# The feed-forward's first product on scaled fp16 parts, with weight sums added by transfers

## The chip, the cores and the metric

The kernel runs on one core of one Trainium2 chip. The metric is the device time of one execution in microseconds (us). The engines of the core are PE (TensorE, the matrix engine; its weight loads are listed apart as PEld), DVE (VectorE), ACT (ScalarE), POOL (GpSimd) and SP (SyncE, which here only starts transfers). POOL starts the transfers that cast a type or add to what lies at the destination; these form the software queue. Those started by SP form the hardware queue.

## The reference

Two layers of an encoder over 1024 tokens of width 1024, then a last norm. All inputs and outputs are fp32.

```python
for l in range(DEPTH):                                   # 2
    h = _rmsnorm(x, g_mix[l])
    p = h @ w_in[l]
    ...                                                  # 8 attention heads, and a gated 31-tap filter
    y = concatenate([y_attn, u], axis=-1) @ w_o[l]
    x = x + y
    h2 = _rmsnorm(x, g_ffn[l])
    z = _dwconv(h2 @ w_up[l], w_dw_ffn[l], b_dw_ffn[l])  # 1024 -> 5632, then 3 taps along the tokens
    zg, zv = split(z, 2, axis=-1)
    x = x + (silu(zg) * zv) @ w_down[l]                  # 2816 -> 1024
return _rmsnorm(x, g_final)
```

`h2 @ w_up` is the feed-forward's first product, the one that changes.

## The kernel before, in words

Each layer runs four stages: input projections, attention, output projection (`wo_steps`), and the feed-forward, which has an up part (`up_steps`) and a down part (`down_steps`). A value is carried as a pair of a high part (the value rounded to a shorter type) and a low part (what is left). A product of two pairs is three matmuls: high by high, high by low, low by high. Before, both parts are fp32r, a 32-bit type that PE takes in one pass.

The first product is cut into 22 blocks `f`, each of 128 channels of the gate and 128 of the value. A block's 2 x 2 halves (gate or value; first or second half of the 1024 input columns) meet the 2 x 2 halves of the activations (rows; first or second 512 tokens) in seven products instead of eight, of sums and differences of halves (Strassen's scheme). `ORDER = (1, 5, 6, 3, 7, 2, 4)` is their order within a block. Each of the seven is twelve matmuls of 128x128 weights by 512 columns: four slices of the input, three matmuls each (`product`, L1120). So the stage has 2 layers x 22 x 7 x 12 = 3696 matmuls.

For each product there must be in time:

- the activations' parts (`self.sets[i]`, tiles `b`): made once a layer in `first`, `combine` and `mix`, at the steps of `MIX_AT`; products 1 and 2 use the plain halves, whose low parts POOL subtracts (`pair`, L1499);
- the weights' parts (tiles `w`): halves that are used as they are (1, 2, 4) arrive by a casting transfer (`cast_pair`, L894), which makes the high part; `complete` then makes the low part by ACT (L189) and an adding transfer (L190). For sums of halves (5, 6, 3, 7) the raw weights `wu` are fetched as fp32 by SP (`fetch`), DVE forms the sums in place by four subtractions or additions (`combine`, L1069), and `part` makes the two parts (L1087, L1497, L1499, L190);
- a free bank of PSUM. `evict` takes the results out by ACT copies and DVE additions into `zg` and `zv`.

After its products, a block goes through the 3-tap filter: `filter_start` is one ACT operation over 1024 tokens (L1505), each `filter_tap` one DVE operation of 1023 columns (L1511), two for the gate (tile `o`) and two for the value (tile `v`); then `silu` on ACT and `close`, a DVE multiplication, whose result is stored by SP. Beside the blocks, `sum_load`, `sum_step` and a store prepare eleven pairs of sums of the down-projection's weights (tiles `sd`, four DVE operations each) from block 7 on.

The order is written out by hand. `feed` walks through the steps; step `n` emits the matmuls of one product (or of two output tiles in `wo_steps`, which has 16 steps), and then everything that was `put` at step `n`, in order of rank. Each engine runs its instructions in this order; only the transfers' places on SP's queue follow from when their waits and buffers allow. So an operation that waits holds up all that stands behind it on its engine. The first four blocks (`LEFT`) are interleaved according to `START`, as the parts of the activations for products 5, 3, 6, 7 and 4 are made only then. From block 4 on (step 44 on) each block takes seven steps.

In `value_squares` and `value_scale` attention finds a power of two as scale for its values: a matmul with ones (tile `vf0p`, L870) sums squares over partitions, and three small DVE operations work on the exponent bits.

Of the kernel before, what the change touches and what calls it, by code (L numbers as in the profile page):

```python
# [71 lines left out]
P_SCALE = 32768.0  # L72
TURNED_BY_DMA = ()
# [17 lines left out]
START += [(i, f + g) for i, g in ((5, 0), (3, 0), (6, 0), (5, 2), (7, 0), (3, 2), (4, 0), (6, 2), (7, 2)) for f in (0, 1)]  # L91
START += [(1, LEFT), (4, 2), (4, 3)]
MIX_AT = (18, 20, 20, 21, 24, 25, 28, 29, 30, 31)
# [3 lines left out]
TAIL_STEPS = 6  # L97
ENDS = (slice(512, 768), slice(768, T))
LEAD_HEADS = 3
FIRST_AT = (0,0,1,1,2,2,3,3)  # L100
EVICT = {(5, 2): 30, (5, 3): 31, (6, 2): 38.295, (6, 3): 39.295, (7, 2): 40.295, (7, 3): 41.295, (5, 0): 24, (5, 1): 25, (1, 2): 35, (1, 3): 36, (2, 2): 36, (2, 3): 37}
# [24 lines left out]
class Encoder:  # L126
# [257 lines left out]
    def run(self):  # L384
# [4 lines left out]
        self.ones = self.cp.tile([128, 128], F32, name="ones")  # L389
        nc.vector.memset(self.ones, 1.0)  # L390
        self.ones_r = self.cp.tile([128, 128], F32R, name="ones_r")
# [9 lines left out]
    def first_sections(self, l, supply):  # L401
# [58 lines left out]
        nc.vector.tensor_copy(out=self.ones_r, in_=self.ones)  # L460
# [87 lines left out]
    def project(self, l, carry):  # L548
# [261 lines left out]
        for i in range(2):  # L810
            held = lambda: launch(query_rope(0), len(seq) - 6)
            add(f"u{i}", "u2", ranked("u2", i, QL, f"u{i}", cqs), lambda i=i: query_rope(1) if i else iter(()), held if i else norm)
        scales = {1: lambda: st.update(squares=self.value_squares(l, w["v"])),
                  2: lambda: st.update(scale=self.value_scale(l, st.pop("squares")))}
# [43 lines left out]
    def value_squares(self, l, w):  # L858
        f = self.cp.tile([128, 8], F32, name=f"vf{l}", tag="vf", bufs=1)
        for k in range(2):  # L860
            t = self.blk(f"vsq{l}_{k}")[:, 0:512]
            self.nc.scalar.activation(out=t, in_=w[0][:, k * 512:(k + 1) * 512].bitcast(F32), func=AF.Square,
                                      scale=self.par[l][:, P_GKV + k:P_GKV + k + 1], accum_out=f[:, k:k + 1])
        return f

    def value_scale(self, l, f):
        nc = self.nc
        ps = self.bank(f"vf{l}p", (128, 1))
        for k in range(2):
            nc.tensor.matmul(ps, self.ones, f[:, k:k + 1], start=k == 0, stop=k == 1)  # L870
        h, s, r = (f[:, i:i + 1] for i in (2, 3, 4))
        nc.vector.tensor_scalar(out=h.bitcast(I32), in0=ps.bitcast(I32), scalar1=24, scalar2=None, op0=ALU.logical_shift_right)
        nc.vector.tensor_scalar(out=s.bitcast(I32), in0=h.bitcast(I32), scalar1=-8388608.0, scalar2=200 * 8388608.0, op0=ALU.mult, op1=ALU.add)
        nc.vector.tensor_scalar(out=r.bitcast(I32), in0=h.bitcast(I32), scalar1=8388608.0, scalar2=39 * 8388608.0, op0=ALU.mult, op1=ALU.add)
        return s, r
# [42 lines left out]
    def load_y(self, l, x, c, k):  # L918
        t = self.blk(f"y{l}_{c}{k}")
        for e in range(2):  # L920
            m = k + 4 * e
            x[m, c] = t[:, HALVES[e]]
            self.nc.sync.dma_start(out=x[m, c], in_=self.xd[l][m][:, HALVES[c]])
# [9 lines left out]
    def wo_steps(self, l, conv, ys, w, casts, x, steps, put):  # L933
        nc, a, par = self.nc, self.a, self.par[l]
        left, right = HALVES
        casts, ps, acc, sq, rf, us = {(1, m): e for m, e in casts.items()}, {}, {}, {}, {}, []
        sets = self.sets = defaultdict(list)

        def load_x():
            for c in range(2):  # L940
                for k in range(4):
                    if (k, c) not in x:
                        self.load_y(l, x, c, k)
# [52 lines left out]
        def norm(c, k):  # L996
            xk = x[k, c]
            nc.vector.scalar_tensor_tensor(out=xk, in0=xk, scalar=par[:, P_GFFN + k:P_GFFN + k + 1], in1=rf[c],
                                           op0=ALU.mult, op1=ALU.mult)

        def first(k):
            norm(0, k)
            i = 1 + k // 4
            sets[i].append(self.pair(x[k, 0], f"b{l}_{i}{k}", "m", True))

        def combine(i, ks, srcs):
            for o, p, q in srcs:
                if q is not None:
                    nc.vector.tensor_tensor(out=o, in0=p, in1=q, op=ALU.subtract)
            pairs = [self.tmp("b", f"b{l}_{i}{k}", F32R, (128, 2, 512)) for k in ks]  # L1010
            for t, src in zip(pairs, srcs):
                nc.scalar.copy(out=t[:, 0], in_=src[0])
            for t, src in zip(pairs, srcs):
                if i in MIX_ADDED:
                    self.complete(None, t[:, 0], t[:, 1], src[0])
                else:
                    nc.vector.tensor_tensor(out=t[:, 1], in0=src[0], in1=t[:, 0].bitcast(F32), op=ALU.subtract)
            sets[i] += pairs
# [23 lines left out]
        for k in range(8):  # L1042
            at = norm_at + FIRST_AT[k]
            put(at, 3, lambda k=k: first(k))
        put(17, 1, lambda: root(1))
        put(18, 0.9, lambda: spread(1))
        b11, b12 = (lambda k, c=c: x[k, c] for c in range(2))
        b21, b22 = (lambda k, c=c: x[k + 4, c] for c in range(2))
        plan = ((5, 0, b11, b12, b11), (3, 4, b22, b22, None), (6, None, b11, b22, b11), (7, None, b12, b22, b12),
                (4, None, b21, b21, b11))  # L1050

        def mix(i, j, o, p, q, ks):
            for k in ks if j is not None else ():
                norm(1, k + j)
            combine(i, ks, [(o(k), p(k), q(k) if q else None) for k in ks])
# [886 lines left out]
```

## Time and profile before

| | us |
|---|---|
| median of 3 runs (2276.03 to 2276.38) | 2276.29 |
| the profiled execution | 2276.63 |
| its span, first to last instruction | 2274.9 |
| up part, first layer (504 to 926) | 422 |
| up part, second layer (1632 to 2052.8) | 420.8 |
| output projection, first layer (406 to 504) | 98 |
| PE busy in the span | 2264.2 |
| DVE busy | 1738.7 |
| ACT busy | 1298.0 |
| POOL busy | 783.0 |

The granted clock of PE was 0.999 over the span. A row of a group of instructions reads: line, engine, operation, tiles written and read (block numbers left out), shapes and type, count, then busy time in us, mean duration in ns, and the idle time of the engine just before them with what ended it. Durations of matmuls overlap, as they are pipelined: the time that one costs is the distance from its start to the next start. DVE's operations overlap a little too.

### The profile page before, as it was taken

How to read it: one execution, taken by the hardware profiler on the slowest of the kernel's cores; microseconds unless marked ns; L12 is line 12 of the kernel's file. 1: busy time of each engine (PE TensorE's matmuls, PEld its weight loads, DVE VectorE, ACT ScalarE, POOL GpSimd, SP SyncE). 2: the span in 40 equal slices, each digit the busy share in tenths (PEclk: the TensorE clock that was granted, in tenths of full speed). 3: DMA queues.
4: the chain of work that ended last, by engine and by line, in shares of the span. 5: the costliest groups of instructions: out<-in, count | busy, mean ns of one | idle time of the engine just before them, and what ended most of it. 6: DMA issues, size and time to landing. Idle time of an engine off the chain costs nothing.

```text
span 2274.9 us, 30440 instructions
## 1 busy us (share of the span) xinstructions
PE 2264.2 (100%) x10690; PEld 1834.8 (81%) x10690; DVE 1738.7 (76%) x2305; ACT 1298.0 (57%) x2058; POOL 783.0 (34%) x812
## 2 busy tenths in 40 slices
PE   9999999999999999999999999999999999999999
PEld 8887777788888888888888877777888888888888
DVE  7989888868877676776559788887697777768765
ACT  5355977646655555544533578784475555555444
POOL 1222797532333333001412237963323333320032
PEclk9999999999999999999999999999999999999999
DMA  6888998856899998935968999867669999989356
GB/s 194 168 180 260 199 207 177 212 151 141 208 281 297 275 297 203 333 106 144 207 139 167 215 255 201 188 150 208 174 132 231 269 300 278 294 208 320 105 121 171
DMA packets 199144, 475.72 MB, mean 209 GB/s; under 512 B 27232, under 2 KB 35280, under 8 KB 198992
## 3 DMA queue, kind: packets, MB, share of 16 engines
q0 software_dynamic: 103136, 222.46, 48.6%
q1 hardware_dynamic: 95568, 250.80, 32.9%
q8 instruction: 84, 1.38, 0.3%
q14 instruction: 68, 0.56, 0.1%
q10 hardware_dynamic: 288, 0.53, 0.1%
HBM read 309.29 MB, written 80.40 MB: 171 GB/s over the span
## 4 chain that ended last, share of the span: by engine, by line
PE 93%; issue 2%; DVE 2%; DMA 1%; ACT 1%; SPq 0%; POOL 0%; DVEq 0%; POOLq 0%; ACTq 0%
PE p L1120 36%; PE pd L1308 18%; PE po L931 7%; PE s L1564 7%; PE t L1604 4%; PE o L1627 4%; PE pq L226 3%; PE pa L226 3%; PE pkv L226 2%; PE pg L226 2%; PE pg L545 2%; PE pa L545 1%; PE pk L226 1%; PE pn L226 1%; PE pkr L759 1%
## 5 line engine op out<-in xcount | busy, mean ns | idle before, releaser
L1120 PE MATMUL p<-b,w 128*128 128x512 f32 x3552 | 807.0, 389 | 0.6 <-DVE zv L1069 0.5
L1120 PEld LDWEIGHTS p<-b,w 128*128 128x128 f32 x3552 | 666.3, 188 | 140.6 <-DVE zv L1069 0.9
L1308 PE MATMUL pd<-ab,wd 128*128 128x512 f32 (+1 forms) x1920 | 422.2, 381 | 0.0
L1308 PEld LDWEIGHTS pd<-ab,wd 128*128 128x128 f32 x1920 | 350.8, 188 | 69.4 <-DVE ab L1499 0.4
L190 POOL DMA_DIRECT2D w<-wu x96 | 84.8, 886 | 360.5 <-ACT w L189 310.0
L1564 PE MATMUL s<-k,q 96*128 96x512 f32 x768 | 207.7, 406 | 0.8 <-ACT p L1574 0.8
L1607 DVE SCALAR_TENSOR_TENSOR pt<-t,pt 128x512 f16<-128x512 f32 x256 | 164.8, 684 | 38.9 <-ACT pt L1606 38.3
L1796 POOL TENSOR_TENSOR late<-gate,par 128x1014 f32<-128x1014 f32 (+12 forms) x79 | 171.6, 2172 | 12.4 <-PE pn L226 12.4
L1606 ACT ACTIVATE pt<-t 128x512 f16<-128x512 f32 x256 | 139.2, 596 | 57.0 <-PE t L1604 56.0
L1511 DVE SCALAR_TENSOR_TENSOR o<-zg,par,o 128x1023 f32<-128x1023 f32 x88 | 112.8, 1283 | 76.5 <-ACT o L1505 75.2
L190 POOL DMA_DIRECT2D w<-in_w_up x116 | 100.5, 867 | 199.2 <-ACT w L189 175.3
L1566 DVE TENSOR_REDUCE mx<-s 128x1 f32<-128x1024 f32 x128 | 155.7, 1217 | 1.3 <-PE s L1564 1.3
L1564 PEld LDWEIGHTS s<-k,q 96*128 96x128 f32 x768 | 135.2, 189 | 23.6 <-ACT p L1574 1.3
L1574 ACT ACTIVATE p<-s,mx 128x1024 f32<-128x1024 f32 x128 | 143.2, 1118 | 4.4 <-DVE mx L1566 4.0
L1779 DVE SCALAR_TENSOR_TENSOR conv<-gate,par,conv 128x1009 f32<-128x1009 f32 (+7 forms) x112 | 142.3, 1274 | 3.7 <-ACT conv L607 1.0
L1604 PEld LDWEIGHTS t<-ident,p 128*128 128x128 f32 x1024 | 119.8, 141 | 25.2 <-DVE yt L1634 0.8
L894 POOL DMA_DIRECT2D wd<-in_w_down x44 | 32.8, 754 | 306.6 <-PE pd L1308 306.4
L1497 ACT CAST ab<-ac 128x512 fp32r<-128x512 f32 x130 | 80.1, 617 | 97.5 <-DVE ac L1243 94.8
L189 ACT ACTIVATE w<-w 128x512 fp32r<-128x512 f32 x212 | 133.5, 630 | 3.0
L1627 PE MATMUL o<-pt,v 128*128 128x512 f16 x512 | 132.8, 381 | 1.2 <-DVE pt L1607 1.1
L1604 PE MATMUL t<-ident,p 128*128 128x128 f32 x1024 | 133.2, 273 | 0.1
L1069 DVE TENSOR_TENSOR zg<-p,zg 128x512 f32<-128x512 f32 x88 | 60.5, 690 | 95.1 <-PE p L1120 88.4
(2117 smaller groups left out, 4083.9 us busy)
## 6 DMA issues: line engine op xcount, KB each, us to landing
w<-in_w_up POOLq DMA_DIRECT2D x232, 256.0 KB, 7.3
wu<-in_w_up SPq DMA_DIRECT2D x88, 512.0 KB, 5.7
w<-wu POOLq DMA_DIRECT2D x96, 256.0 KB, 5.9
sd<-in_w_down SPq DMA_DIRECT2D x44, 512.0 KB, 9.9
ws<-sd SPq DMA_DIRECT2D x44, 512.0 KB, 7.0
wd<-in_w_down POOLq DMA_DIRECT2D x88, 256.0 KB, 5.4
act<-v SPq DMA_DIRECT2D x36, 512.0 KB, 5.8
ac<-act SPq DMA_DIRECT2D x72, 256.0 KB, 6.1
```

Of the source, the lines that this page charges most:

```text
L190: self.nc.gpsimd.dma_start(out=lo, in_=src, accum_op=ALU.add)
L226: nc.tensor.matmul(ps[:, HALVES[c]], w, x[:, HALVES[c]], start=(k == 0 and s == 0), stop=(k == n - 1 and s == 2))
L931: self.nc.tensor.matmul(ps, p[:, sl], q[:, cs], start=(k == 0 and t == 0), stop=(k == 3 and t == 2))
L1120: nc.tensor.matmul(ps, w[p][:, k * 128:(k + 1) * 128], b[:, q], start=(i in (1, 5, 2) and k == 0 and t == 0), stop=(k == 3 and t == 2), sk ...
L1308: nc.tensor.matmul(ps[t, m][:, cs], w[i, j][p][:, m * 128:(m + 1) * 128], b[:, q, cs], start=(i in (1, 5, 2) and j == 0 and s == 0), stop= ...
L1564: nc.tensor.matmul(ps[:, cs], q[i][0:96, qs], k[j][0:96, cs], start=(s == 0), stop=(s == 2))
L1566: nc.vector.tensor_reduce(out=mx, in_=ps, op=ALU.max, axis=AX.X, negate=True)
L1574: nc.scalar.activation(out=p, in_=ps, func=AF.Exp, bias=mx, accum_out=st["sums"][:, qt:qt + 1])
L1604: nc.tensor.transpose(tp[:, i, qi * 128:(qi + 1) * 128], st["p"][2 * qp + qi][:, kt * 128:(kt + 1) * 128], self.ident)
L1607: nc.vector.scalar_tensor_tensor(out=lo, in0=tp, scalar=P_SCALE, in1=hi, op0=ALU.mult, op1=ALU.subtract)
L1627: nc.tensor.matmul(po, v[2 * c + i][:, h // 2, e, :], pt[s][:, 2 * (c % 2) + i, :], start=(c == 0 and i == 0 and s == 0), stop=(c == 3 and ...
L1796: self.nc.gpsimd.tensor_tensor(out=p[:, lo:hi], in0=u[:, lo + s:hi + s], in1=self.tap(l, j, t).broadcast_to([128, hi - lo]), op=ALU.mult)
```

## The change

- The parts of activations and weights for the seven products are fp16 instead of fp32r. The weights are multiplied by a power of two per block before they are split, the activations by one per layer (`gs`, from the norm's gains); the results are multiplied back in `evict` (`back`, and `nback` where the sign is turned).
- The power of two of a block comes from its sum of squares: ACT squares both raw halves with an accumulator (`own_squares`), one fp32 matmul with ones sums over partitions (`own_total`, a matmul of two columns in PE's stream), and five small DVE operations work on the exponent bits (`own_scale`). The first four blocks share one such matmul a layer (`first_total`), within the output projection. Attention's `value_scale` becomes `scales`, with one matmul and more small operations.
- The raw weights of all halves are fetched by SP. Sums of halves are made in place by four adding transfers a block on POOL (`sum5`, `sum6`, `sum3`, `sum7`) instead of DVE operations. High parts are ACT operations with a scale (`upper`), low parts DVE operations with a scale (`lower`); there are no casting transfers and no `complete` in this stage.
- Signs of some sums are turned, so that additions do; `evict` and the down part's `combine` and `evict` follow.
- Activations: tiles of rows `2k` and `2k+1` lie side by side, so that one operation makes parts of two; their low parts are all DVE's.
- `START` is reordered: products 1 and 2 of blocks 0 to 3, then 5, 3, 6, 7 and 4, each of blocks 0 to 3. `MIX_AT` and `EVICT` follow. The filters of blocks 0 to 3 start at the steps of `TAPS_AT`: 36, 39, 42, 46 (gate) and 44, 48, 52, 57 (value). `SUM_AT` sets the down sums' steps after product 1.

The places in the order for block `f` of 4 and above, in steps from its first product: fetch -18, squares -15 and -14, total -13, its scale -12, then high and low parts by `UP`.

```diff
+START += [(i, f) for i in (5, 3, 6, 7, 4) for f in range(LEFT)]
...
+TOTAL_AT = 32
+TAPS_AT = (36, 39, 42, 46), (44, 48, 52, 57)
+UP = {'fetch': -18, 'squares': -15, 'total': -13, 1: (-2, -2), 5: (-10, -9), 6: (-5, -4), 3: (0, 1), 7: (2, 3), 4: (-1, 0)}
+SUM_AT = (0, 1, 2, 6)
...
+        def begin(i, e, src, tag):
+            two = self.tmp(tag, f"b{l}_{i}{e}", F16, (128, 2, 2, 512))
+            src = src.rearrange("p (e c) -> p e c", e=2)
+            nc.scalar.copy(out=two[:, :, 0], in_=src)
+            half[i, e] = two, src
+            sets[i] += [two[:, e] for e in range(2)]
+
+        def end(i, e):
+            two, src = half.pop((i, e))
+            nc.vector.tensor_tensor(out=two[:, :, 1], in0=src, in1=two[:, :, 0], op=ALU.subtract)
...
-        def combine(f, o, p, q, op=ALU.subtract):
-            z = quarters(f)
-            sub(z[o], z[p], z[q], op)
...
+        def block(f, e, h):
+            return a["w_up"][l, f + e * NF][:, HALVES[h]]
+
+        def add_in(dst, src):
+            nc.gpsimd.dma_start(out=dst, in_=src, accum_op=ALU.add)
+
+        def sum5(f):
+            add_in(raw[f][1][:, left], block(f, 1, 1))
...
+        def squares(f, e, out):
+            t = self.blk(f"wsq{l}_{f}{e}", F16)
+            nc.scalar.activation(out=t, in_=raw[f][e], func=AF.Square, accum_out=out)
+
+        def scales(ps, out, w):
+            ps = ps.rearrange("p (f e) -> p f e", e=2)
+            scale, back, nback, v, h = (out[:, i * w:(i + 1) * w] for i in range(5))
+            nc.vector.tensor_reduce(out=v, in_=ps, op=ALU.add, axis=AX.X)
+            self.half_exponent(h, v)
+            self.power(scale, h, -1.0, 204.0)
...
+        def first_total():
+            ps = self.bank(f"wt{l}", (128, 2 * LEFT))
+            tags = self.banks[1][0]
+            tags.insert(0, tags.pop())
+            nc.tensor.matmul(ps, self.ones, st["sums"], start=True, stop=True)
...
+        def own_total(f):
+            st["total", f] = self.pp.tile([128, 2], F32, name=f"wt{l}_{f}", tag=f"d{6 + (f > LEFT and (f + 1) % 2)}", bufs=1)
+            nc.tensor.matmul(st["total", f], self.ones, st["sums", f][:, 6:8], start=True, stop=True)
...
+        def upper(t, src, f):
+            nc.scalar.activation(out=t, in_=src, func=AF.Copy, scale=scale[f])
+
+        def lower(t, src, hi, f):
+            nc.vector.scalar_tensor_tensor(out=t, in0=src, scalar=scale[f], in1=hi, op0=ALU.mult, op1=ALU.subtract)
...
         def evict(i, f):
-            z = st[f]
+            z = zs[f]
+            by = nback[f] if i in (5, 7, 4) else back[f]
+            copy = lambda o, src: nc.scalar.activation(out=o, in_=src, func=AF.Copy, scale=by)
+            plus = lambda o, src: nc.vector.scalar_tensor_tensor(out=o, in0=src, scalar=by, in1=o, op0=ALU.mult, op1=ALU.add)
...
         for f in range(LEFT, NF):
-            n = at[1, f]
+            n = m = at[1, f]
             for e in range(2):
-                put(n - 8, 5, lambda f=f, e=e: fetch(f, 1 - e))
-            put(n - 5, 3, lambda f=f: combine(f, 0, 0, 2))
-            put(n - 4, 3, lambda f=f: combine(f, 2, 2, 3, ALU.add))
...
+                at_step(m + UP["fetch"], 5 + e / 10, fetch, f, e, "b" if e else "wr")
+                at_step(m + UP["squares"] + e, 2, own_squares, f, e)
+            at_step(m + UP["squares"] + 1, 2.1, sum5, f)
+            at_step(max(m + UP["total"], TOTAL_AT), 0.4, own_total, f)
+            at_step(max(m + UP["total"], TOTAL_AT) + 1, 0.5, own_scale, f)
+            for i in (5, 6, 3, 7, 4):
+                hi, lo = (max(m + o, TOTAL_AT + 1) for o in UP[i])
+                at_step(hi, 3.6, part_hi, i, f)
+                at_step(lo, 3.7 if hi == lo else 3.5 if i != 6 else 1, part_lo, i, f)
+                if i in (5, 6):
+                    at_step(lo, 3.75, (sum6, sum3)[i - 5], f)
+            at_step(n + UP[1][0], 1, first_hi, f)
+            at_step(n + UP[1][1], 2, first_lo, f)
+            at_step(n + UP[1][1] + 1, 2, sum7, f)
+            at_step(m + 3, 9, raw.pop, f)
```

299 lines of the change are left out of this document (169 added, 130 removed).

## The prediction, made before the changed kernel was run

> **What bounds the kernel now.** I read the page first (busy shares, slices, the chain that ended last), then the busy time by stretch, then the instructions in order of time. Each engine's row gives busy time, share of the span, and instructions.
>
> ```profile
> PE 2264.2 (100%) x10690; PEld 1834.8 (81%) x10690; DVE 1738.7 (76%) x2305; ACT 1298.0 (57%) x2058; POOL 783.0 (34%) x812
> PE 93%; issue 2%; DVE 2%; DMA 1%; ACT 1%; SPq 0%; POOL 0%; DVEq 0%; POOLq 0%; ACTq 0%
> PE p L1120 36%; PE pd L1308 18%; PE po L931 7%; PE s L1564 7%; PE t L1604 4%; PE o L1627 4%; PE pq L226 3%; PE pa L226 3%; PE pkv L226 2%; PE pg L226 2%; PE pg L545 2%; PE pa L545 1%; PE pk L226 1%; PE pn L226 1%; PE pkr L759 1%
> L1120 PE MATMUL p<-b,w 128*128 128x512 f32 x3552 | 807.0, 389 | 0.6 <-DVE zv L1069 0.5
> L1120 PEld LDWEIGHTS p<-b,w 128*128 128x128 f32 x3552 | 666.3, 188 | 140.6 <-DVE zv L1069 0.9
> 504.00:926.00 422.00, 421.40 (x1862) 348.11 (x1861) 313.84 (x404) 244.08 (x374) 125.38 (x165) 1.00 0.92 245
> 1632.00:2052.80 420.80, 420.80 (x1862) 348.12 (x1862) 314.00 (x404) 244.09 (x374) 123.95 (x165) 1.00 0.92 246
> ```
>
> The stage that changes is the up-projection, L1120. The last two rows are its two passes: length, then busy time of PE, PEld, DVE, ACT and POOL, granted clock, DMA share. PE is busy throughout and stands still 0.6 us before a matmul of L1120 in the whole run. So PE's spacing sets the stage, and whatever else is hidden stays hidden only while its turn comes in time: DVE is at 74% of the pass, DMA at 92%.
>
> **What one matmul costs.** These are instructions in order of time: start, length, engine, line, count.
>
> ```profile
> 298.86 1.02 PE L1627 MATMUL o<-pt,v 128*128 128x512 f16 x4
> 299.72 0.71 PE L1604 MATMUL t<-ident,p 128*128 128x128 f32 x5
> 699.68 4.70 PE L1120 MATMUL p<-b,w 128*128 128x512 f32 x20
> L1627 PEld LDWEIGHTS <-v 128*128 128x128 f16 x512 | 41.7, 98 | 64.3 <-issue 29.2 <-DVE yt L1634 1.0 <-DVE pt L1607 0.6
> ```
> ```profile
> 190.73 0.61 PE L226 MATMUL pn<-cqs_2l,wu10h 128*128 128x512 f32 x2
> 191.18 0.50 PE L870 MATMUL vf0p<-vf,ones 128*128 128x1 f32 x4
> 191.54 0.72 PE L226 MATMUL pn<-cqs_0h,wu10h 128*128 128x512 f32 x2
> 191.92 0.15 DVE L872 TENSOR_SCALAR vf<-vf0p 128x1 int32<-128x1 int32 x1
> 192.10 0.63 PE L226 MATMUL pn<-cqs_0h,wu10l 128*128 128x512 f32 x2
> ```
>
> Twenty matmuls of L1120 take 4.70 us, the last alone 0.389: (4.70-0.389)/19 = 0.2269 us from start to start. Four fp16 matmuls of the same shape start at 298.86 and the next work at 299.72: 0.86/4 = 0.215 us, by the rounding of the starts 0.2125 to 0.2175. I take 0.216. Between 190.73 and 192.10 lie four such fp32r matmuls (0.908) and two fp32 matmuls (four records): 1.37-0.908 = 0.462, so 0.231 us for one fp32 matmul with one or two columns. DVE reads its result 0.24 us after it ended (191.68 to 191.92).
>
> **The change, part by part.**
>
> *Products in fp16.* 2 layers x 22 blocks x 7 products x 12 = 3696 matmuls by 0.2269-0.216 = 0.0109: **-40.3 us**, all on the path. A weight load is 98 ns in fp16 against 188 here; both are shorter than the matmul. Bounds: 0 if long runs stay at 0.227, -53 at 0.2125. I take the fp16 row, being of the same shape.
>
> *Totals for the scales.* 18 blocks a layer each get one fp32 matmul in PE's stream: 36 x 0.231 = **+8.3 us**. Five small DVE operations follow it (0.15 each, row 191.92), 0.75 a block, and two squares on ACT. The first four blocks share one total in the output-projection stage; the next bank there waits for DVE to read it, 0.24+0.15+0.06 = 0.45, with 0.23 for the matmul; the attention's scale takes one matmul instead of two (-0.23). **+0.9** for both layers.
>
> *Weight sums and parts.* Gone: four DVE subtractions a block (L1069 `wu`) and the casting transfers with their corrections; new: four adding transfers a block into the raw weights, ACT makes every high part and DVE every low part. POOL issues four instead of eight. Durations and spacings of DVE:
>
> ```profile
> 701.12 0.69 DVE L1069 TENSOR_TENSOR wu<-wu,wu 128x512 f32<-128x512 f32 x1
> 701.72 1.28 DVE L1511 SCALAR_TENSOR_TENSOR v<-zv,par,v 128x1023 f32<-128x1023 f32 x1
> 702.92 0.69 DVE L1069 TENSOR_TENSOR sd<-sd,sd 128x512 f32<-128x512 f32 x1
> 703.52 0.69 DVE L1069 TENSOR_TENSOR wu<-wu 128x512 f32<-128x512 f32 x1
> L1069 DVE TENSOR_TENSOR v<-v,o 128x1024 f32<-128x1024 f32 x44 | 53.6, 1217 | 0.1
> L998 DVE SCALAR_TENSOR_TENSOR y<-y,par,rf 128x512 f32<-128x512 f32 x16 | 11.3, 745 | 4.0 <-ACT rf L993 4.0
> L1505 ACT ACTIVATE o<-zg,par 128x1024 f32<-128x1024 f32 x44 | 54.2, 1232 | 15.4 <-DVE zg L1069 12.4 <-DMA w<-wu 2.6 <-DMA ws<-sd 0.4
> L1574 ACT ACTIVATE p<-s,mx 128x1024 f32<-128x1024 f32 x128 | 143.2, 1118 | 4.4 <-DVE mx L1566 4.0
> L1574 ACT ACTIVATION_READ_ACCUMULATOR p<-s,mx 128x1 f32 x128 | 26.8, 209 | 0.0
> ```
>
> Successive starts give 0.60 us for 512 columns and 1.20 for a tap; a scaled one (745 long) then 0.66, a product of 1024 columns 1.14. A steady block after: five low parts 3.3, the pair of products 1 and 2 1.2, three evictions 1.98, four taps 4.8, closing 1.14, scale 0.75 = 13.2; with the down-projection's sums (4 x 0.60) 15.6. PE takes 84 x 0.216+0.23 = 18.37 a block (19.06 now). DVE stays under it in sum, but two chains are tight.
>
> (1) Product 7's low part. Its DVE turn, from the end of the total's matmul: 0.24 to the read, 0.75 scale, tap 1.2, sum 0.6, low part of 6 of the next block 0.66, tap 1.2, itself 0.75 = 5.4, gaps 0.1. PE needs it two products of 2.59 later plus two matmuls of 0.216, 5.6. It fits by 0.1 in blocks with sums, by 0.7 in others: at most 0.2 a block, 0 to 4 us over 22 such blocks.
>
> (2) A loop through the raw weights' buffer: product 7's low part frees it, the transfer of three blocks ahead goes in (L), ACT squares it (about 1.25 from start to start, of 1.118 and 0.209), ACT starts the gate's filter of this block behind that (1.23), and DVE has from its first tap to the next low part of 7: four taps 4.8, four low parts 2.64, an eviction 0.66, scale 0.75, three sums 1.8 = 10.65. Together 13.1+L, against 18.37: it waits where L is over 5.2 us (7.0 without sums). L by issue, with the stretch each is from (share of DMA in the rows after):
>
> ```profile
> wu<-in_w_up SPq DMA_DIRECT2D x88, 512.0 KB, 5.7
> w<-wu POOLq DMA_DIRECT2D x96, 256.0 KB, 5.9
> ```
> ```profile
> wu<-in_w_up SPq DMA_DIRECT2D x9, 512.0 KB, 6.3
> q0 software_dynamic: 5671, 10.34, 53.6%
> q1 hardware_dynamic: 4668, 16.98, 49.7%
> ```
> ```profile
> wu<-in_w_up SPq DMA_DIRECT2D x4, 512.0 KB, 5.3
> 650.00:742.00 92.00, 92.00 (x407) 76.17 (x407) 67.12 (x85) 50.74 (x77) 27.75 (x36) 1.00 1.04 298
> 850.00:905.00 55.00, 55.00 (x245) 45.54 (x244) 38.07 (x46) 29.67 (x46) 16.31 (x22) 1.00 0.84 212
> ```
>
> The 6.3 is from 650 to 742, with DMA at 1.04; the 5.3 from 850 to 905, at 0.84. After the change the software queue moves 1 MB a block instead of 2; its five adds and three casts fill 53.6% now, so four adds fill 27% (if a cast costs the same) to 43% (if casts cost nothing); the plain transfers stay near 52% of the shorter block. That makes 0.79 to 0.95, and I take the lower half, 0.84. So I take L = 5.3 as the middle: half of 22 blocks are later, by perhaps 0.5 us (from the 1.0 between the two medians): 11 x 0.5 = **+5.5 us**, chain (1) within it. Ends: 0 (L never above 5.2) and 22 x 1.1 = +24 (L stays 6.3).
>
> The queues: on SP the transfer that waits for its buffer has the loads of the down-projection's sums and the stores of finished blocks behind it; the stores are read only in the next stage. On POOL each add waits for a DVE low part and has the next adds behind it. From the low part to the next high part lie four products (10.4) for the sums of 6 and 3, three (7.8) for 7, against an issue of 0.9 and the 5.9 us of `w<-wu`: spare 3.6 and 1.0, and 7's own low part comes a product later. Nothing, unless an add takes over 8 us.
>
> [...]
>
> *Order, and taps put off.* The first four blocks' filters move behind product start: in steps 47 to 56 (ten products, 25.9 us of PE) DVE has ten taps 12, four closings 4.6, five evictions 3.3, nine widths of low parts 6.0 to 7.0, a scale 0.75: 26.7 to 27.6 by spacings, about 30 by full durations. It falls 1 to 4 us behind, and since low parts of products 6 and 7 queue behind those taps, PE waits for them. I take 3.5 a layer, **+7 us**; ends 0 (slack of the steps before) and 12.
>
> *Activations' parts, evictions with scales, paired loads.* The POOL subtractions go to DVE (the second row: busy times of the first output projection):
>
> ```profile
> L1499 POOL TENSOR_TENSOR b<-y,b 128x512 fp32r<-128x512 f32 x16 | 24.2, 1625 | 28.1 <-ACT b L1497 28.1
> 406.00:504.00 98.00, 97.29 (x452) 78.83 (x451) 67.30 (x104) 46.36 (x74) 38.73 (x42) 1.00 0.67 184
> ```
>
> Two of those become one DVE operation of 1.2 us at the stage's start; PE's spacing there (2.59 a product) leaves DVE about 2 us ahead, so I cost it at nothing; uncovered it would be 4 x 1.2 a layer. The eight early squares on ACT (1.25 each) lie in the output projection, where ACT is busy 46 of 98 us; nothing either, uncovered 1 us.
>
> Sum, against the profiled execution's own 2276.63 (span 2274.9 and 1.7 around it, 0.34 above the median of the runs): -40.3+8.3+0.9+5.5+7 = -18.6, so **2258.0 us**.
>
> **Rivals.**
>
> *No waits.* DVE and transfers always arrive: -40.3+8.3+0.9 = -31.1, so 2245.5. For it: before, PE stands only 0.6 us on L1120 although DMA is full. Against: DVE has less room now.
>
> *The buffer loop decides (slower).* In blocks with sums the period becomes 13.1+L. The gain, 31.1 less 7 = 24, is spent when it exceeds 18.37 by 24/22 = 1.1, at L = 6.4; at L = 7.3 it costs 22 x 2.03 = 45, giving 2245.5+7+45 = 2297. For it: the 6.3 median with sums, DMA full there. Against: a MB less a block.
>
> *The put-off taps cost much more*: one product's time (2.59) lost in each of blocks 4 to 6 beyond my 7, 15.5 in both layers: 2273.5. For it: 30 us of DVE work by durations against 25.9; against: 26.7 by spacings.
>
> *No faster stream* (the change doesn't do what it says). Long fp16 runs keep 0.227: 2276.6+8.3+0.9 = 2285.8, and up to 12.5 of waits, fewer in longer blocks: 2290. Against: only runs of four, but hundreds of them, all near 0.215.
>
> [...]
>
> **How the numbers follow.** My case (5 to 20 us of waits) 0.52; no waits 0.18; taps 0.12; loop 0.12; no faster stream 0.05; the page's 131 ns 0.01. A difference under 0.2% is 4.6 us, about what separates a change from none here. My case and no waits lie below 2271.7, as does a third of the taps' case and the 0.01; the loop's case is slower in most of its range and within the bound in the rest, as is the taps' case. So faster 0.79, same 0.06, slower 0.15. The range leaves out a last tenth on either side: 2243 to 2281.
>
> **What would show it.** L1120's spacing near 0.216 with weight loads near 98 ns. One two-column matmul a block, 0.23 us each. Idle time of PE before the products: some 12 us, released by DVE low parts, in the first 60 us of the stage (7) and in blocks with sums (5.5); DVE waits for the gate's filter start, ACT for `wu` transfers. I am wrong if that idle time exceeds 30 us, if landing in the sum blocks stays over 6 us, or if waits stand in the output projection.

## The result, and the profile after

The changed kernel takes 2266.23 us (median of 5 runs, 2263.01 to 2266.99) against 2276.29 before (5 runs, 2276.03 to 2276.78). The ratio is 0.9953, with a 95% interval of 0.9938 to 0.9967: 10 us faster, where 18 were forecast. The profiled execution took 2264.85.

First the page of the changed kernel: busy times of the engines, the chain that ended last, and the groups that answer to those of before.

```profile
span 2263.0 us, 30127 instructions
PE 2233.7 (99%) x10762; PEld 1511.4 (67%) x10762; DVE 1809.0 (80%) x2484; ACT 1349.5 (60%) x2076; POOL 659.2 (29%) x632
...
PE 71%; DVE 12%; DMA 8%; ACT 4%; issue 4%; POOL 1%; SPq 0%; DVEq 0%; POOLq 0%; ACTq 0%
PE pd L1417 18%; PE p L1221 18%; PE s L1677 7%; DMA wu<-in_w_up 5%; PE po L956 5%; PE t L1717 4%; PE o L1740 4%; PE pa L234 2%; DVE w L1185 2%; DVE v L1624 2%; PE pg L234 2%; PE pg L552 2%; DVE conv L1892 2%; PE pq L234 1%; DVE sd L1102 1%
L1221 PE MATMUL p<-b,w 128*128 128x512 f16 x3696 | 807.6, 379 | 16.6 <-DVE w L1185 12.1
L1221 PEld LDWEIGHTS <-w 128*128 128x128 f16 x3696 | 360.3, 99 | 449.0 <-DVE w L1185 22.5
```

The products are L1221 now. Their share of the chain fell from 36% to 18%: DVE's low parts, the filter's taps and the transfers of the raw weights stand in the chain in their place. That alone is no lost time, since the chain runs through whatever ended last. Lost time is where PE stands, and this is in the list of PE's waits (engine, line, who ended the wait; us in total, times, longest):

```profile
PE p L1221 <- DVE w L1185: 12.1, 15, 1.6
PE p L1221 <- ACT zg L1228: 3.0, 3, 1.3
PE s L1677 <- DVE qn L748: 3.0, 1, 3.0
PE p L1221 <- DVE b L1034: 1.3, 2, 0.6
...
PE po L956 <- DVE wt L1133: 0.5, 2, 0.3
```

Before, PE stood 0.6 us on the products. Idle time counts from a matmul's modelled end; the time lost, from start to start, is some 0.16 us more each (a matmul of the products is listed as 0.379 us long, and the next starts after 0.216). Below I give lost time from the starts of all 3696 matmuls.

Where the time went can be read from the stage's ends (first and last start of its matmuls in the first layer, and in both):

```profile
L1221 PE MATMUL p<-b,w x1848: 376/379/390, 507.1 to 919.9; 128*128 128x512 f16 x185
...
L1221 PE MATMUL p<-b,w x3696: 376/379/390, 507.1 to 2040.3; 128*128 128x512 f16 x195
```

The first layer's stage takes 412.8 us (421.6 before), the second's, from 1627.7, 412.6 (420.4 before): 16.6 us less in both. Outside of the stage the span grew by 4.7 us; 2274.9-16.6+4.7 = 2263.0. Split by the prediction's terms, in us:

| term | forecast | measured |
|---|---|---|
| fp16 instead of fp32r, 3696 matmuls | -40.3 | -42.1 |
| 36 totals | +8.3 | +5.0 |
| taps put off (waits of blocks 4 to 6) | +7 | +7.2 |
| waits of blocks 7 to 18 but 13 | +5.5 | +7.5 |
| a late add, block 13 | 0 | +4.2 |
| low parts of activations, block 0 | 0 | +1.6 |
| outside of the stage | +0.9 | +4.7 |
| sum | -18.6 | -11.9 |

A total costs 0.14 us of PE's stream. Its two records start at 719.34, the next product's matmul at 719.48, where it would have started at 719.34 without them:

```profile
719.34 0.28 PE L1161 MATMUL wt<-wf,ones_r 128*128 128x2 f32 x2
719.48 1.89 PE L1221 MATMUL p<-b,w 128*128 128x512 f16 x8
```

The first measured term is what is left of the stage's 16.6 when the others are taken off. Of it, 40.3 is the spacing (0.2159 us where nothing waits, 0.2268 before); the rest is mostly 2.0 us that the stage before lost at 13 uneven starts.

Three places show the kinds of wait. These are instructions of the changed kernel in order of time (start, length, engine, line, what; in brackets the idle time and who ended it). At 594.64 PE waits 1.6 us for a low part that stands behind a closing multiplication (L1102) and a put-off tap (L1624):

```profile
591.50 1.22 DVE L1102 TENSOR_TENSOR v<-v,o 128x1024 f32<-128x1024 f32 x1
592.64 1.28 DVE L1624 SCALAR_TENSOR_TENSOR o<-zg,par,o 128x1023 f32<-128x1023 f32 x1
593.83 0.75 DVE L1185 SCALAR_TENSOR_TENSOR w<-wu,wf,w 128x512 f16<-128x512 f32 x1
594.64 1.68 PE L1221 MATMUL p<-b,w 128*128 128x512 f16 x7 [1.60 <-DVE w L1185]
```

One turn of the loop through the raw weights' buffer, from product 7 of block 11 to that of block 12, stands at 725 to 745. A low part of product 7 ends at 725.01, the transfer is issued at 725.08, ACT waits for its landing with the square, behind the square wait the gate's filter and DVE's taps, and behind those the next low part of product 7, for which PE waits:

```profile
724.26 0.75 DVE L1185 SCALAR_TENSOR_TENSOR w<-wu,wf,w 128x512 f16<-128x512 f32 x1
725.08 0.33 SPq L1106 DMA_DIRECT2D wu<-in_w_up  x1
732.76 1.06 ACT L1128 ACTIVATE wsq<-wu 128x1024 f16<-128x1024 f32 x1 [8.13 <-DMA wu<-in_w_up]
733.82 1.22 ACT L1618 ACTIVATE o<-zg,par 128x1024 f32<-128x1024 f32 x1
735.07 1.28 DVE L1624 SCALAR_TENSOR_TENSOR o<-zg,par,o 128x1023 f32<-128x1023 f32 x1 [3.68 <-ACT o L1618]
...
744.33 0.74 DVE L1185 SCALAR_TENSOR_TENSOR w<-wu,wf,w 128x512 f16<-128x512 f32 x1
745.13 1.04 PE L1221 MATMUL p<-b,w 128*128 128x512 f16 x4 [0.86 <-DVE w L1185]
```

The turn takes 20.06 us (725.01 to 745.07), 7.68 of them from the issue to the square. The other 12.4 go beside 18.28 for a block of PE's stream (84 x 0.2159 and a total), so the loop should make PE wait where issue to square takes over 5.9 us. It does, within 0.2 us and block 13 apart: in the first layer that time was 6.2 to 7.7 us ahead of the five blocks that wait there (9, 12, 16, 17, 18) and 4.6 to 6.1 ahead of six that don't (7, 8, 10, 11, 14, 15); in the second layer 5.9 to 7.2 ahead of six and 5.0 to 5.7 ahead of five.

The third place lies outside of the stage, at the start of the first layer's attention. PE's wait there is 3.0 us; the rows are the changed kernel's, DVE and POOL:

```profile
192.16 0.14 DVE L887 COPY sc<-sc0p 128x3 f32<-128x3 f32 x1
...
193.31 0.15 DVE L897 TENSOR_SCALAR sc<-sc 128x1 f32<-128x1 f32 x1
...
195.69 6.03 DVE L752 SCALAR_TENSOR_TENSOR qn<-qn,qns 128x1024 fp32r<-128x1024 f32 x2
195.47 2.06 POOL L1909 TENSOR_TENSOR late<-gate,par 128x1023 f32<-128x1023 f32 x1 [5.71 <-DMA q<-rc]
198.44 2.19 POOL L1909 TENSOR_TENSOR late<-gate,par 128x1020 f32<-128x1020 f32 x1
202.91 0.97 PE L1677 MATMUL s<-k,q 96*128 96x512 f32 x3 [3.00 <-DVE qn L748]
```

And the kernel before, the same two DVE operations:

```profile
194.56 4.05 DVE L745 SCALAR_TENSOR_TENSOR qn<-qn,qns 128x1024 fp32r<-128x1024 f32 x2
195.57 1.96 POOL L1796 TENSOR_TENSOR late<-gate,par 128x1023 f32<-128x1023 f32 x1 [6.04 <-PE pn L226]
```

The pair starts 1.1 us later than before, 0.9 of them for ten small operations in place of three. So each of its two parts now starts under a POOL operation (195.47 and 198.44), where before the first had started ahead of it, and they took 6.03 us instead of 4.05. One such operation alone takes 1.22 (start 189.65 in the kernel before).

The wait has a second price: for 3.41 us behind it PE's granted clock was a half. These rows are two stretches of the changed kernel (length, then busy time of PE, PEld, DVE, ACT and POOL, granted clock, DMA share, GB/s):

```profile
201.14:204.56 3.42, 1.65 (x7) 1.38 (x8) 2.25 (x3) 1.61 (x3) 2.81 (x1) 1.00 1.07 280
204.56:207.97 3.41, 3.41 (x10) 2.63 (x9) 3.41 (x8) 2.51 (x8) 0.00 (x0) 0.50 1.01 402
```

From the first of attention's matmuls `s` to the eleventh it takes 5.38 us here, against 3.75 before. Some of this is made good later: at the first matmul `po` of the output projection the changed kernel is 2.4 us behind (422.05 against 419.64). The two output projections take 1.6 us longer together (1.4 forecast); the other 0.7 are spread.

### The profile page after: what moved, and what is told of

It is laid out like the page before. It is cut to its first block, busy times and chain, and to the rows that moved or that the text cites. A ratio compares the mean times of both kernels' runs of the same rounds, so it can differ in the third digit from the quotient of the medians.

```text
span 2263.0 us, 30127 instructions
## 1 busy us (share of the span) xinstructions
PE 2233.7 (99%) x10762; PEld 1511.4 (67%) x10762; DVE 1809.0 (80%) x2484; ACT 1349.5 (60%) x2076; POOL 659.2 (29%) x632
## 4 chain that ended last, share of the span: by engine, by line
PE 71%; DVE 12%; DMA 8%; ACT 4%; issue 4%; POOL 1%; SPq 0%; DVEq 0%; POOLq 0%; ACTq 0%
PE pd L1417 18%; PE p L1221 18%; PE s L1677 7%; DMA wu<-in_w_up 5%; PE po L956 5%; PE t L1717 4%; PE o L1740 4%; PE pa L234 2%; DVE w L1185 2%; DVE v L1624 2%; PE pg L234 2%; PE pg L552 2%; DVE conv L1892 2%; PE pq L234 1%; DVE sd L1102 1%
## 5 line engine op out<-in xcount | busy, mean ns | idle before, releaser
L1221 PE MATMUL p<-b,w 128*128 128x512 f16 x3696 | 807.6, 379 | 16.6 <-DVE w L1185 12.1
L1221 PEld LDWEIGHTS <-w 128*128 128x128 f16 x3696 | 360.3, 99 | 449.0 <-DVE w L1185 22.5
L1112 POOL DMA_DIRECT2D wu<-in_w_up x176 | 153.7, 945 | 757.2 <-DVE w L1185 370.4
L1128 ACT ACTIVATE wsq<-wu 128x1024 f16<-128x1024 f32 x88 | 92.3, 1050 | 179.8 <-DMA wu<-in_w_up 159.3
L1185 DVE SCALAR_TENSOR_TENSOR w<-wu,wf,w 128x512 f16<-128x512 f32 (+1 forms) x216 | 177.4, 834 | 14.6 <-ACT w L1182 14.6
L1182 ACT ACTIVATE w<-wu,wf 128x512 f16<-128x512 f32 (+1 forms) x216 | 162.5, 783 | 6.9 <-DMA wu<-in_w_up 6.8
L1624 DVE SCALAR_TENSOR_TENSOR o<-zg,par,o 128x1023 f32<-128x1023 f32 x88 | 112.6, 1280 | 53.9 <-ACT o L1618 53.7
```

What stands on the lines that cost most here:

```text
L1182: nc.scalar.activation(out=t, in_=src, func=AF.Copy, scale=scale[f])
L1185: nc.vector.scalar_tensor_tensor(out=t, in0=src, scalar=scale[f], in1=hi, op0=ALU.mult, op1=ALU.subtract)
L1221: nc.tensor.matmul(ps, w[p][:, k * 128:(k + 1) * 128], b[:, q], start=(i in (1, 5, 2) and k == 0 and t == 0), stop=(k == 3 and t == 2), sk ...
L1624: self.nc.vector.scalar_tensor_tensor(out=o[:, a:b], in0=z[:, at + a:at + b], scalar=self.par[l][:, tap:tap + 1], in1=o[:, a:b], op0=ALU.m ...
```

## The experiments

The kernel before was timed beside all of them; its medians then were 2276.8 to 2277.3. Waits are us lost from start to start, both layers together, in each profiled execution; matmuls at a lowered clock are in them.

| kernel | median, us | ratio to before, 95% | block 0 | blocks 4-6 | blocks 7-18 |
|---|---|---|---|---|---|
| changed | 2266.23 | 0.9938 to 0.9967 | 1.6 | 7.2 | 11.7 |
| squares behind | 2258.33 | 0.9905 to 0.9932 | 1.6 | 8.5 | 3.6 |
| late scales | 2261.47 | 0.9917 to 0.9942 | 1.6 | 7.2 | 11.1 |
| no first taps | 2258.70 | 0.9902 to 0.9929 | 1.6 | 1.9 | 10.3 |
| squares behind and late scales | 2255.16 | 0.9890 to 0.9917 | 1.6 | 8.5 | 2.7 |
| taps behind | 2264.44 | 0.9932 to 0.9957 | 1.6 | 7.5 | 11.1 |
| sums without a gap | 2261.47 | 0.9924 to 0.9951 | 1.6 | 7.2 | 7.9 |
| all five edits | 2252.74 | 0.9881 to 0.9908 | 0.3 | 13.9 | 0.4 |
| taps not put off | 2275.18 | 0.9983 to 1.0001 | 1.9 | 18.8 | 9.8 |
| four edits | 2251.11 | 0.9875 to 0.9902 | 0.3 | 9.0 | 1.9 |
| four, taps spread | 2250.42 | 0.9870 to 0.9897 | 0.3 | 8.1 | 1.5 |
| four, values later | 2259.18 | 0.9909 to 0.9936 | 0.3 | 17.0 | 2.1 |

**Squares behind the filter start.**

```diff
-                at_step(m + UP["squares"] + e, 2, own_squares, f, e)
-            at_step(m + UP["squares"] + 1, 2.1, sum5, f)
+                at_step(m + UP["squares"] + e, 3.2, own_squares, f, e)
+            at_step(m + UP["squares"] + 1, 3.3, sum5, f)
```

> Edit: in blocks 4 and above ACT's squares of the raw weights stand behind the start of the gate's filter in the same step instead of ahead of it. Theory of the buffer loop (low part of product 7 frees the raw buffer, transfer, square, filter start, taps, next low part): the filter no longer waits for the transfer, so the waits at the third matmul of product 7 in blocks 7 to 18, 11 us over both layers in the changed kernel, fall to the 4 us that stand at block 13; about 2259. Rival, DVE's own turn (scale, taps, sums, low parts) is what is late: the waits stay and the time with them, 2266. Third: the total's matmul now waits for the squares instead: up to 40 totals by 0.5 us, 2275 or more.

It took 2258.33, 7.9 less. In this kernel the filter start (here of block 12) comes first and waits for an eviction instead of the transfer, and the square is not late:

```profile
749.75 1.24 ACT L1618 ACTIVATE o<-zg,par 128x1024 f32<-128x1024 f32 x1 [6.20 <-DVE zg L1229]
750.89 1.04 ACT L1128 ACTIVATE wsq<-wu 128x1024 f16<-128x1024 f32 x1
```

The transfers are no faster. This is the line on landing of the raw weights' transfers between 640 and 870, for the changed kernel and then for this one:

```profile
DMA to landing us min/median/max: 5.2/6.1/7.6
```
```profile
DMA to landing us min/median/max: 6.1/6.3/7.2
```

(The view gives the landing of five of the 24 transfers in each.) So it is the loop: every wait of blocks 7 to 18 went except those at block 13, with the transfers no shorter than before. The rival falls: DVE's own turn fits into the block. So does the third: totals that wait for the squares would have made it slower. Block 5 waits 1.4 us more than before; the record does not show why.

**Late small operations of the attention's scale.** Three DVE operations stay behind the matmul, on two columns; the rest moves to the start of the output projection.

```diff
-        ps = self.bank(f"sc{l}p", (128, 3))
-        nc.tensor.matmul(ps, self.ones, f[:, 0:3], start=True, stop=True)
...
+        for k in range(2):
+            nc.tensor.matmul(ps[:, 0:1], self.ones, f[:, k:k + 1], start=k == 0, stop=k == 1)
+        nc.tensor.matmul(ps[:, 1:2], self.ones, f[:, 2:3], start=True, stop=True)
...
+        put(0, 5.5, lambda: self.late_scales(l))
```

> Edit: of the small DVE operations behind the attention's scale only three stay there, as before the change; the others run at the start of the output projection; PE makes three matmuls of one column there instead of one of three. Theory: the 3.0 us for which PE stands at the start of the first layer's attention come from those operations (1.2 us of DVE, which put its next operations under a long POOL operation); they go, less 0.9 for four matmuls more: 2264. Rival: POOL's operation holds DVE there whatever stands ahead: 2267.

It took 2261.47, 4.8 less by the medians and 2.9 by the two profiled executions. The wait is gone, and the half clock behind it too (the granted clock is 1.000 over the span), which the theory had not counted: from the first `s` to the eleventh it takes 3.70 us. The pair of operations takes 2.35 us. Its second part starts at 196.11, 0.04 us ahead of the POOL operation, and this time POOL's is the one that takes longer, 2.93 us instead of 2.06:

```profile
194.97 2.35 DVE L752 SCALAR_TENSOR_TENSOR qn<-qn,qns 128x1024 fp32r<-128x1024 f32 x2
196.15 2.93 POOL L1915 TENSOR_TENSOR late<-gate,par 128x1023 f32<-128x1023 f32 x1 [6.20 <-PE pn L234]
200.44 1.55 PE L1683 MATMUL s<-k,q 96*128 96x512 f32 x6
```

So the rival, that POOL's operation holds DVE whatever stands ahead, falls, but by a narrow margin. What a different order of the two starts costs is shown further down.

**No first taps.** This kernel leaves out the outer taps of the filters of blocks 0 to 3.

```diff
+            if f >= LEFT:
                 put(n + 1, 3, lambda f=f: filter_tap(f, 0, 0))
                 put(n + 2, 3, lambda f=f: filter_tap(f, 0, 2))
...
+            if f >= LEFT:
                 put(m + 1, 3, lambda f=f: filter_tap(f, 1, 0))
                 put(m + 2, 3, lambda f=f: filter_tap(f, 1, 2))
```

> Edit: leaves out the two outer taps of the filters of blocks 0 to 3 (gate and value), 32 DVE operations of 1.2 us over both layers. Theory of the taps put off: the 3.5 us a layer at product 7 of blocks 4 to 6 are the queue behind those taps and go whole: 2259. Rival: those waits come from the raw weights' transfers or adds of these blocks: less than 2 us off, 2264 or more.

It took 2258.70, and the waits of blocks 4 to 6 fell from 7.2 to 1.9 us. So most of them come from DVE's queue, not from the transfers.

**Squares behind and late scales together.** Both diffs above.

> Edit: squares behind the filter start and late small operations together. If both theories hold, their gains add, 7 and 2: about 2257. If DVE's turn is the bound in the blocks with sums and POOL the bound at the attention's start: 2266.

It took 2255.16: 11.1 less than the changed kernel, where the two alone took off 7.9 and 4.8. The gains nearly add.

**Taps behind the low parts.** With the work of the taps kept, can their place be mended?

```diff
-            put(n + 1, 3, lambda f=f: filter_tap(f, 0, 0))
-            put(n + 2, 3, lambda f=f: filter_tap(f, 0, 2))
+            r = 3 if f >= LEFT else 3.8
+            put(n + 1, r, lambda f=f: filter_tap(f, 0, 0))
+            put(n + 2, r, lambda f=f: filter_tap(f, 0, 2))
...
+            put(max(m + 3, n + 5), r, lambda f=f: close(f))
```

> Edit to the changed kernel: the taps and the closing multiplication of blocks 0 to 3 stand behind the low parts of the same step on DVE instead of ahead of them; nothing is left out. Theory (place in the queue): the waits at product 7 of blocks 4 to 6, 3.6 us a layer, come from one or two such operations standing ahead of a low part, and at most 1 a layer is left: 2261. Rival (amount of work): DVE has more work than time in steps 47 to 56, so the waits only move, to evictions and the next block's parts: 2265 or more.

2264.44, between the two; by the waits the rival holds. The wait at block 4 (3.5 us in both layers) went, and block 6 got 4.1 where it had 0.5. The sum of the three is 7.5 instead of 7.2: an amount of work, not a place.

**Sums without a gap.**

```diff
-            n = at[1, 7 + j * 13 // 11]
+            n = at[1, 7 + j]
             put(n - 4, 5, lambda j=j: sum_load(j))
```

> Edit to the changed kernel: the sums of the down-projection's weights belong to blocks 7 to 17 one after the other, instead of leaving out block 13. In the changed kernel a late add (10.2 us to landing, median 5.1) is issued 0.7 us ahead of two 512 KB loads for those sums, which come only there right behind the adds; PE then waits 2 us at block 13 in both layers. Theory: without the gap no add lands after 8 us and the waits at block 13 go: 2262, or 2264 if block 13 now has the small wait of any block with sums. Rival: the add is late for another reason: 2266.

2261.47. The slowest add between 640 and 870 landed in 8.3 us (10.2 in the changed kernel; 8.6 and 10.3 in the second layer), and block 13 waits 1.4 us in both layers together instead of 4.2. That the gap makes the add late is shown; that the loads issued right behind it do so is read from the order of the issues alone. In the changed kernel the late add is issued at 751.2, and ACT's high part of product 7 waits until 761.4; an eviction stands behind that, and PE behind the eviction:

```profile
761.38 1.33 ACT L1182 ACTIVATE w<-wu,wf 128x512 f16<-128x512 f32 x2 [2.83 <-DMA wu<-in_w_up]
...
763.57 0.67 ACT L1228 ACTIVATE zg<-p,wf 128x512 f32<-128x512 f32 x1
764.28 0.59 PE L1221 MATMUL p<-b,w 128*128 128x512 f16 x2 [1.15 <-ACT zg L1228]
```

**All five edits.** Those of squares, scales, taps and gap, and the low parts of the first activations ahead of the weights' in their step:

```diff
-                put(n + 1, 0.5, lambda i=i, e=e: end(i, e))
+                put(n + 1, 0.1, lambda i=i, e=e: end(i, e))
```

> Edit: squares behind the filter start, late small operations, taps behind low parts, sums without a gap, and the low parts of the first activations ahead of the weights' in their step. If each works on its own wait: 2255.2 (the first two together) less 5 (taps) less 2.5 (late add) less 1.2 (activations) = 2246.5. If DVE's amount of work bounds the steps after the first four blocks: 2251 or more.

2252.74, 6 us above the forecast. Block 0 and blocks 7 to 18 wait almost nothing, but blocks 4 to 6 lose 13.9 us, so the alternative holds (2251 or more): the taps' edit moved the waits together, and then the clock fell to a half, in both layers (0.998 over the span). The rows give busy times by stretch of this kernel, as before, with the granted clock third from the end:

```profile
627.73:631.15 3.42, 1.57 (x7) 0.50 (x6) 3.42 (x6) 2.37 (x4) 0.87 (x1) 1.00 0.61 180
631.15:634.56 3.41, 3.41 (x10) 1.22 (x8) 1.36 (x2) 0.00 (x0) 0.00 (x0) 0.50 0.96 251
634.56:637.97 3.41, 3.41 (x17) 1.53 (x16) 2.96 (x4) 0.15 (x1) 0.68 (x2) 1.00 0.28 112
```

**Taps not put off.** This undoes one part of the change.

```diff
-TAPS_AT = (36, 39, 42, 46), (44, 48, 52, 57)
+TAPS_AT = (37, 40, 37, 40), (42, 43, 44, 45)
```

> Edit to the changed kernel: the filters of blocks 0 to 3 are not put off, they start at about the steps of the kernel before (gate 37, 40, 37, 40; value 42 to 45). Theory that putting them off is what costs 3.6 a layer: 2259. Rival, that the work is only moved and was put off for room: waits of 2 to 8 us a layer stand at products of steps 38 to 50 instead, 2263 to 2275.

2275.18, as slow as the rival's upper end: 9 us more than with the taps put off. The waits of blocks 4 to 6 all stand at block 4 now, 18.8 us in both layers, and again the clock fell behind the longest:

```profile
600.46 11.77 PE L1221 MATMUL p<-b,w 128*128 128x512 f16 x46 [5.10 <-DVE w L1185]
```
```profile
597.05:600.46 3.41, 0.00 (x0) 0.00 (x1) 3.41 (x5) 0.00 (x0) 0.87 (x1) 1.00 0.34 53
600.46:603.87 3.41, 3.41 (x9) 1.21 (x10) 1.74 (x2) 0.00 (x0) 0.00 (x0) 0.50 1.04 382
```

Putting the taps off is thus worth 9 us, at 7.2 us of waits that stay.

**Four edits.** All but the taps behind the low parts.

> Edit: the four edits that each took a wait away (squares behind the filter start, late small operations, sums without a gap, the first activations' low parts ahead), without the taps behind the low parts. Theory: the half granted clock after the waits of blocks 5 and 6 in the run with all five edits came from moving the taps; without it blocks 4 to 6 wait 3.9 us a layer as in the run with the first two edits, block 13 nothing, block 0 0.2: 2255.2 less 2.5 less 1.3, so 2251. Rival: the taps' edit helped within the sum of all five: 2254 or more.

2251.11, as the theory says, and no stretch of the stage has a lowered clock (1.000 over the span). The medians of this and the kernel with all five are 1.6 us apart, less than the runs of either differ, so the medians alone don't tell; the waits of blocks 4 to 6 (9.0 against 13.9) do.

**Four edits, taps spread.**

```diff
-TAPS_AT = (36, 39, 42, 46), (44, 48, 52, 57)
+TAPS_AT = (36, 38, 40, 44), (43, 47, 54, 59)
```

> Edit: the same four, and the filters of blocks 0 to 3 at steps 36, 38, 40, 44 (gate) and 43, 47, 54, 59 (value), so that two taps and two closings leave steps 47 to 56. Theory (amount of DVE work in those steps): 4.7 us less work there against 4 lacking, the waits of blocks 4 to 6 fall to under 1 a layer: 2245. Rival: ACT, busy without a break from step 41 to 47, is late with the filter starts and high parts, and waits of 2 to 4 a layer stand at blocks 3 and 4: 2250.

2250.42, the lowest median: 1.2% faster than before (ratio 0.9883, 0.9870 to 0.9897) and 15.8 us faster than the changed kernel. It can't be told from the four edits alone, 0.7 us above it, as the runs of either differ by more. The theory falls in its size, too. The wait at block 4 fell from 3.5 to 1.4 us in both layers and that of block 5 from 4.5 to 1.3, but block 6 has 5.4 (1.0 before that edit). The rival is wrong too: nothing waits at block 3.

**Four edits, values later.**

```diff
-TAPS_AT = (36, 39, 42, 46), (44, 48, 52, 57)
+TAPS_AT = (36, 39, 42, 46), (43, 47, 53, 60)
```

> Edit: the same four, the gates' filters of blocks 0 to 3 as in the changed kernel (36, 39, 42, 46) and the values' at 43, 47, 53, 60. One closing leaves steps 47 to 56 and block 3's taps move three steps back. Theory (amount of work): waits of blocks 4 to 6 fall by the 1.1 of a closing and by what block 0's earlier taps take off: 2248. Rival: as for the other edit, 2250 or more.

2259.18, 8 us slower than the four alone, where the theory said 3 faster. Waits of blocks 5 and 6 grew to 15.8 us, with the clock at a half behind two of them in the first layer (0.998 over the span). Why three steps more for block 3 cost that much isn't settled; evictions on ACT (`zg`, 4.1 us in PE's waits, none with the four) became late, so it isn't DVE's amount of work alone.

## Why the prediction was right or wrong

The time lies in the range (2243 to 2281) and on the forecast side, 8 us above the forecast (2266.2 against 2258.0).

- *fp16 products*: right. Long runs keep the short runs' spacing, 0.2159 us; the rival of no faster stream is out. No run shows the 131 ns that the prediction gives a chance of 0.01; the stage's spacing stands in its place. The spacing alone is worth the 40.3 forecast. The term is 1.8 us larger, since the uneven starts of the stage before are gone too.
- *Totals*: right in kind, too large in size: 0.14 us each instead of 0.231. The row that 0.231 was read from had two such matmuls behind one another, and the matmul behind them also started 0.1 us late. The first total's wait in the output projection stands there as forecast (0.5 us in both layers, `wt` in the list of waits).
- *Taps put off*: right, 7.2 against 7, and for the reason given: low parts of product 7 queue behind taps, DVE has more work than time in those steps. Leaving out the taps removes 5.3 of it, and changing their places mostly moves it. They stand 87 to 126 us after the stage's start, not in its first 60 us.
- *Buffer loop*: right in mechanism; that the size is near (7.5 against 5.5) is luck. Two errors nearly cancel. The landing took longer than the 5.3 us assumed (median from issue to square in blocks 8 to 18: 6.1 us in the first layer, 5.9 in the second). And the loop had more room than assumed: it waits above 5.9 us, not 5.2, as the rest of it takes 12.4 us and not 13.1. With 6.1 in the prediction's own sum, it would have been some 19 us. The sign "landing in the sum blocks stays over 6 us" came true in the first layer without the sum being wrong for it. Taking the filter start out of the loop removed the waits and left the landing time.
- *Late add*: the step that failed is "Nothing, unless an add takes over 8 us". One add a layer took over 10, behind the gap of the sums, where the loads for the next sums come right behind the adds. Block 13 lost 4.2 us, of which 1.4 stay without the gap. The median that I used does not tell of the slowest one in each layer.
- *Activations*: "I cost it at nothing" was wrong by 1.6 us. DVE was behind at the second product of the stage; putting the low part one place ahead took 1.3 of it away.
- *Attention's scale*: I counted only its matmul (-0.23). The small operations after it are seven more on DVE's queue, ahead of the work that attention's first product waits for: PE stands 3.0 us, and then the clock is a half for 3.41 us. Beside the late add this is the largest error, and it is a step that I did not follow: DVE's queue at a place outside of the stage.

So the 6.7 us between -18.6 and -11.9 hide errors of both signs: PE's own work came out 5 us cheaper than forecast, the rest, nearly all of it waits, 12 us dearer.

The rival that none waits (2245.5) is where the edits lead: 2250.4 with the four edits and the spread taps, where 8 of some 10 us of waits are still those of the put-off taps.

Early in the stage, at 549.51, with DMA at 0.42 between 545 and 565, a 512 KB transfer of the raw weights landed in 3.2 us; from 640 to 870, with DMA at 0.86, the median is 6.1 and the fastest 5.2. Against the loop's 5.9 us, it waits by these figures in the later stretch.

## What to carry to other kernels

When the engine that sets the time gets faster, chains of the other engines that just kept up with it begin to hold it up. So work out, block by block, the loops that go through a buffer, a transfer and back, and look at which instruction stands ahead of which on the engine that waits, as one change of order there was worth 8 us beside the 10 of the whole change. An operation that waits for a transfer belongs behind those that don't. Small operations at a place that looks free are not free if the next in the queue is what the bounding engine waits for.

## What the runs showed of the hardware

Two things I had not expected. The first is after which waits the granted clock of PE fell to a half (0.50 in the rows above; in the changed kernel's attention the matmuls `pv` then start 0.43 us apart, at 205.13, 205.56 and 205.99, against 0.227 ahead of the wait). It fell not only after a wait of 5.1 us but after one of 3.0 in the changed kernel's attention, and after two waits of 0.55 and 1.29 us (idle time) within three microseconds, in the run with all five edits:

```profile
628.50 0.59 PE L1227 MATMUL p<-b,w 128*128 128x512 f16 x2 [0.55 <-ACT zg L1234]
630.38 4.45 PE L1227 MATMUL p<-b,w 128*128 128x512 f16 x12 [1.29 <-DVE w L1191]
```

With values later, waits alike in both layers were followed by it in the first layer and not in the second at block 5:

```profile
606.68:610.10 3.42, 1.45 (x7) 0.41 (x5) 3.42 (x5) 2.54 (x4) 0.88 (x1) 1.00 0.40 49
610.10:613.51 3.41, 3.41 (x9) 1.22 (x8) 2.77 (x3) 0.00 (x0) 0.00 (x0) 0.50 0.64 179
1726.26:1729.67 3.41, 1.56 (x7) 0.43 (x5) 3.41 (x5) 2.82 (x4) 0.86 (x1) 1.00 0.30 36
1729.67:1733.08 3.41, 3.28 (x16) 1.51 (x17) 3.41 (x5) 0.00 (x0) 0.00 (x0) 1.00 0.72 187
```

In the rows of four runs each stretch at half the clock is 3.41 us long; the rows of the second layer are laid in the same steps (326 of 3.4133 us from 613.51 to 1726.26). In the 3.41 us ahead of a half clock PE was busy 0.00 us (597.05 to 600.46), 1.45, 1.57 and, in attention, where the matmuls have another shape, 1.65; behind 1.56 us (1726.26 to 1729.67) the clock stayed at 1.00. PE's busy time, as the profile models it, doesn't tell the two cases apart here: 1.56 lies between 1.45 and 1.57. Why like waits were followed by half the clock once and once not was not shown.

The second: two DVE operations that take 2.35 us together took 4.05 and 6.03 when a POOL operation on two tensors ran beside them. In the places shown, the one that started second took longer. Where POOL was first, DVE's operation ended 1.08 us after POOL's (198.61 after 197.53 in the changed kernel), close to the 1.22 that it takes alone. Where DVE was first by 0.04 us, it took 1.22 and POOL's took 2.93. (Two more DVE operations, at 199.63 with the late scales and at 1323.01 in the changed kernel, started 0.35 us ahead of such a POOL operation and took 3.65 and 3.63 all the same; POOL was issuing a transfer as they started.) The profiled execution with four edits has the same instructions there as the late scales, but POOL came first by 0.09 us:

```profile
196.08 2.91 DVE L752 SCALAR_TENSOR_TENSOR qn<-qn,qns 128x1024 fp32r<-128x1024 f32 x1
195.99 1.92 POOL L1915 TENSOR_TENSOR late<-gate,par 128x1023 f32<-128x1023 f32 x1 [6.08 <-PE pn L234]
```

By the 25th matmul `s` that execution had lost 1.5 us against the one with the taps spread (16.48 us from the first, against 15.00). The kernel before, where POOL was first too, took 16.53. DVE is on the path there, and the start of a POOL operation was part of the price, 1.5 us between these two.
